# Modulation products of a two-block transformer kernel: units of 1 MB and pairs of 2 MB, and the stages beside which they stand

## The chip, the core and the metric

The kernel runs on one core of a Trainium2 chip. The metric is the device time of one execution in microseconds; three runs were taken of the kernel before, and one execution was profiled by itself. The engines are TensorE (PE, with its weight loads as PEld), VectorE (DVE), ScalarE (ACT), GpSimd (POOL) and SyncE (SP, which issues nearly all the transfers).

## What is computed

Two transformer blocks of two layers each work on 256 latent tokens and, in the first layer, on 256 context tokens of width 1024. Each layer takes six modulation vectors from a conditioning vector: a product with a 1024 x 6144 matrix, 24 MB in float32. Cut to what matters here:

```python
def modulation(cond, w_ada, b_ada):
    m = jax.nn.silu(cond) @ w_ada + b_ada
    return [t[..., None, :] for t in jnp.split(m, 6, axis=-1)]

for i in range(DEPTH):                       # first block
    sh1, sc1, g1, sh2, sc2, g2 = modulation(c, w_ada[i], b_ada[i])
    h = modulate(rms_norm(x, norm1_g[i]), sh1, sc1)
    x = x + g1 * (mixer(h) @ w_out[i])       # windowed, differential attention, gMLP
    x = x + g2 * conv_ffn(modulate(rms_norm(x, norm2_g[i]), sh2, sc2),
                          w_up[i], conv_w[i], conv_b[i], w_down[i])

for i in range(DEPTH):                       # second block
    m = (sc @ w_mod[i] + b_mod[i]).reshape(B, N_MOD, D_MODEL)
    # layer 0: attention with 8 heads; layer 1: multi-scale pooling
    # then conv_ffn_2, each behind a modulated norm and gated
```

The modulation weights of all four layers are 96 MB, a third of what the kernel reads.

## The kernel before

Everything is kept with features on the partitions: `x` is 128 x 8 x 256. Every other product is made of float32 weights split into a high and a low part: `fetch` (L203) loads a 1 MB chunk, ACT casts it to the high part (L238), DVE subtracts for the low part (L240), and `mms` (L270) issues three products per tile (high by high, high by low, low by high: L285, L286, L289). The modulation product is done in plain float32 and needs no split.

**The stages.** The first layer runs its mixer and its feed-forward for both streams (512 columns), the second layer and the second block for the latent stream alone (256 columns). Each feed-forward (`ffn`, L986) has 22 up-projections, each followed by a convolution (L978, L981, L983; in the first block of both the gate and the value half), and down-projections in groups that are interleaved with the ups.

**The modulation units.** A unit (`mod_part`, L400) is a quarter of one of the six vectors: 1 MB of weights, eight matmuls with 32 stationary columns (L410) into four quarters of one accumulator `acc`. They show in the trace as 16 records. The quarter's sum is put into `msum`: copied by ACT for the first quarter (L414), added by DVE for the others (L416). After the fourth, two transposes (L425) and one addition (L427) write the vector. `acc` is a PSUM tag with two buffers, which the down-projections, the output projections and the projections of the mixers use too, in turn.

**Their loads.** `mod_load` (L362) takes either one 1 MB buffer of the pool `x8` (seven buffers of 8 KB per partition, shared with activations and with every third split weight chunk), or two of three half-megabyte buffers `mw`. `mod_units` (L431) makes a list of steps: step q issues the matmuls of unit q - `ahead` and then the load of unit q.

**What sets the order.** PE and SP run in the program's order (`manual_schedule`, L1360). `spread` (L80) puts a list of steps evenly between the steps of a stage; `Line` (L33) holds generators with costs and due times, and lets their second halves follow when they are due. SP issues transfers in order, and each waits until its buffer has been read. Beside which stage the units stand is written in four places: `fill_a` (L1323), beside the first layer's mixer; `fill_f` (L1330), beside a feed-forward; the line `if l == 1` in `block1` (L945), beside the second layer's mixer; and `attention2` (L1241), beside the second block's attention. The last twelve units of the fourth layer stand in `self.late` (L1443).

```python
def fill_f(self, i):
    if i == 0:
        return self.more_units((1, 0, 12), x8=True)
    return self.more_units((2, 8, 24)) if i == 1 else []
...
        if l == 1:
            seq = seq[:12] + spread(seq[12:], self.more_units((1, 12, 24), (2, 0, 8)))
```

Of the kernel before, what the change touches and what calls it, by code (L numbers as in the profile page):

```python
# [79 lines left out]
def spread(main, fill):  # L80

    out, done = [], 0
    for i, u in enumerate(main):
        out.append(u)
        want = len(fill) * (i + 1) // len(main)
        out += fill[done:want]
        done = want
    return out + fill[done:]
# [3 lines left out]
WAIT = dict(b00=6, b01=5, b10=5.5, b_pv=2.5, c00=5, c01=5, c10=5, c_norm=1.5, c_pv=4,   # L92
            gmlp=3.5, gmlp_end=2, mod=1, norm=1.2, norm1=3, pool_out=4.5, qk0=4,
            qk0_first=10, qk1=4, qk1_first=8, qk2=4, s=6, s_pv=1.5)
# [11 lines left out]
class Stack:  # L106
# [201 lines left out]
    def go(self, gen, name=None):  # L308
        self.n += 1
        name = name or f"#{self.n}"  # L310
        self.line.start(name, gen)
        return name
# [84 lines left out]
        nc.vector.tensor_tensor(m, m, b.unsqueeze(2).to_broadcast([P, 2, 2]), ALU.add)  # L397
        yield 0.22, 0

    def mod_part(self, i, n, then=None):  # L400


        nc = self.nc
        j, q = divmod(n, 4)
        cpad = self.cpad
        acc = self.psum("acc", [P, 512])[:, :256]
        w = self.wm.pop((i, n))
        for e in range(2):
            for u in range(4):
                nc.tensor.matmul(acc[32 * u:32 * u + 32], lhsT=cpad[:, 2 * q + e], rhs=w[e][:, 256 * u:256 * u + 256],  # L410
                                 start=e == 0, stop=e == 1)
        if q == 0:
            self.msum[i, j] = self.mp.tile([P, NT], F32, tag="msum", name="msum", bufs=1)
            nc.scalar.copy(self.msum[i, j], acc)  # L414
        else:
            nc.vector.tensor_tensor(self.msum[i, j], self.msum[i, j], acc, ALU.add)  # L416
        if then is not None:
            then()
        yield 0.9, WAIT["mod"] if q == 3 else 0
        if q < 3:  # L420
            return
        sb = self.msum.pop((i, j))
        tr = self.psum("tr", [P, 2, 4, 32])
        for t in range(2):
            nc.tensor.transpose(tr[:, t].rearrange("p u v -> p (u v)"), sb[:, P * t:P * t + P], self.ident)  # L425
        b = self.sm(f"sm{i}", "b")[:, KD * j:KD * j + KD].rearrange("p (u t) -> p t u", t=2)
        nc.vector.tensor_tensor(self.mod[i][:, j].rearrange("p (u t) v -> p t u v", t=2), tr[:, :, :, i // 2 * 2:i // 2 * 2 + 2],  # L427
                                b.unsqueeze(3).to_broadcast([P, 2, 4, 2]), ALU.add)
        yield 0.22, 0

    def mod_units(self, ns, x8=False, ahead=1):  # L431

        def step(q):
            load = (lambda: self.mod_load(*ns[q], x8)) if q < len(ns) else (lambda: None)
            if q >= ahead:
                yield from self.mod_part(*ns[q - ahead], load)
            else:
                load()

        return [lambda q=q: self.go(step(q), "m%d.%d" % ns[q - ahead] if q >= ahead else None)  # L440
                for q in range(len(ns) + ahead)]

    def mods(self, i, j):

# [251 lines left out]
    def block1(self, l, after):  # L696
        nc, key, line = self.nc, f"sm{l}", self.line
# [4 lines left out]
        t = self.x8("kvqc")  # L702
        kTB, vB = t[:, 0:512], t[:, 512:1024].rearrange("p (k c) -> p k c", k=4)
        qTC = t[:, 1024:2048].rearrange("p (s a t) -> p s a t", s=2, a=2)
        t = self.x8("kvc")
# [3 lines left out]
        u, gk = uv[:, 0], f"gn{l}"  # L709
# [17 lines left out]
        def chunk(ci, post, ss):  # L727
            return [lambda s=s: self.go(self.proj(f"win{l}", ci, s, post), f"c{ci}{s}") for s in ss]
# [184 lines left out]
        need = lambda *names: [lambda: line.ensure(*names)]  # L913
        rev = streams[::-1]
        fill = self.fill_a(l)
        seq = chunk(0, post_bkv, (0,)) + chunk(1, post_bq(0), (0,)) + chunk(0, post_bkv, (1,))
        if l == 0:
            seq += chunk(1, post_bq(0), (1,))
        else:
            seq = seq[:2] + need("n1") + [self.last_loads] + seq[2:]  # L920
# [4 lines left out]
        n = len(streams)  # L925
# [16 lines left out]
        for a, b in MOVES[l]:  # L942
            seq.insert((a + b) % len(seq), seq.pop(a % len(seq)))
        if l == 1:
            seq = seq[:12] + spread(seq[12:], self.more_units((1, 12, 24), (2, 0, 8)))  # L945
        for u_ in seq:
            u_()
        if l == 1:
# [232 lines left out]
    def attention2(self):  # L1181
        nc, i, line = self.nc, 2, self.line
        kT, v = self.kT, self.v2
        self.qk_wait = WAIT["qk2"]
        qT = self.x8("qT").rearrange("p (a t) -> p a t", a=8)
        t = self.sx[:, 4:8].rearrange("p k t -> p (k t)")
# [50 lines left out]
        need = lambda *names: [lambda: line.ensure(*names)]  # L1237
        kx, vx = chunk(0, lambda acc, s: self.post_k(acc, s, tk)), chunk(1, self.post_v)
        q = [chunk(2 + c, post_q(c)) for c in range(4)]
        un = units()  # L1240
        f = self.more_units((3, 0, 12), x8=True, ahead=2)  # L1241
        seq = f[:1] + kx + vx + f[1:2] + q[0] + q[1] + need("c0", "c1", "c2")
        seq += spread(un[0], f[2:5]) + q[2] + need("c3") + spread(un[1], f[5:8]) + q[3] + need("c4")
        seq += spread(un[2], f[8:11]) + need("c5") + spread(un[3], f[11:])
        seq += need(*(f"a{hp}1" for hp in range(4)))
        for u in seq:
            u()
# [82 lines left out]
    def fill_f(self, i):  # L1330

        if i == 0:
            return self.more_units((1, 0, 12), x8=True)
        return self.more_units((2, 8, 24)) if i == 1 else []

    def more_units(self, *parts, **kw):
        return self.mod_units([(i, n) for i, a, b in parts for n in range(a, b)], **kw)
# [278 lines left out]
```

## Time and profile before

| | us |
|---|---|
| three runs, median (lowest to highest) | 1776.91 (1774.46 to 1777.22) |
| the profiled execution, its own time | 1774.65 |
| its span in the trace | 1772.9 |
| PE busy in the span | 1618.3 (91%) |
| DVE busy | 1195.8 (67%) |
| ACT busy | 878.9 (50%) |
| POOL busy | 135.2 (8%) |
| read from memory | 285.21 MB, 161 GB/s over the span |

The stages, by the first and last instructions of each: the first layer's mixer to 323 us, the first feed-forward 323 to 722, the second layer's mixer 722 to 941, the second feed-forward 941 to 1163, the second block's attention 1163 to 1301, the third feed-forward 1317 to 1500, the pooling mixer to 1570 and the fourth feed-forward to the end. A busy share is an average over a stretch in which matmuls overlap, so a stage with PE at 98% may still issue slowly; the granted clock of a stretch (PEclk) is 1.00 at 2.4 GHz and 0.50 at 1.2 GHz. What a stage waits for is read from its own waits, and not from the shares.

### The profile page before, as it was taken

Reading aid. Unit: us, or ns where it says so; the run is one execution under the profiler, and the core shown is the slowest. Engines: PE = TensorE matmul, PEld = TensorE weight load, DVE = VectorE, ACT = ScalarE, POOL = GpSimd, SP = SyncE. Lnnn points to the kernel's source line nnn. Section 1 sums busy time; section 2 is a strip of 40 time slices with the busy share of each in tenths; the row PEclk is TensorE's granted clock in tenths of the full one; section 3 lists DMA queues with packets and bytes.
Section 4 is the critical chain, followed back from the end, with each engine's and each line's share of the span. In section 5 each row is a group of like instructions: output and inputs, shape, how many; then the busy total and the mean of one; then the engine's idle time right before and its main releaser. Section 6 shows DMA issues by size and latency. Waiting matters only on the chain.

```text
span 1772.9 us, 32420 instructions
## 1 busy us (share of the span) xinstructions
PE 1618.3 (91%) x12604; PEld 1427.0 (80%) x12604; DVE 1195.8 (67%) x2903; ACT 878.9 (50%) x2147; POOL 135.2 (8%) x162
## 2 busy tenths in 40 slices
PE   7999797999999999898879999998979999779997
PEld 5878456989899898875468898886769999569997
DVE  5775786755564557876667768676786567886565
ACT  5343654533332343455345556454556565656563
POOL 0000001000000000000000001000141011431110
PEclk9999898999999999898989999999989999889998
DMA  7344331334333422245645776657455546435452
GB/s 308 119 143 143 124 107 49 130 109 142 113 127 120 142 97 98 89 139 203 227 143 192 254 256 233 209 189 263 166 182 188 176 176 210 179 119 212 157 187 87
DMA packets 71435, 288.36 MB, mean 163 GB/s; under 512 B 8177, under 2 KB 9457, under 8 KB 62577
## 3 DMA queue, kind: packets, MB, share of 16 engines
q1 hardware_dynamic: 69696, 283.91, 46.3%
q10 hardware_dynamic: 1584, 2.38, 0.4%
q8 instruction: 99, 1.62, 0.4%
q14 instruction: 56, 0.45, 0.1%
HBM read 285.21 MB, written 1.05 MB: 161 GB/s over the span
## 4 chain that ended last, share of the span: by engine, by line
PE 63%; DVE 17%; DMA 10%; ACT 6%; issue 3%; POOL 1%; SPq 0%; ACTq 0%; DVEq 0%; POOLq 0%
PE S L285 9%; PE S L286 9%; PE S L289 9%; PE acc L285 8%; PE acc L286 8%; PE acc L289 8%; DVE wl L240 5%; DMA w<-in_wup_dram 4%; PE acc L410 3%; DMA w<-in_wdn_dram 2%; ACT wh L238 2%; PE tr L661 2%; DVE ht L519 1%; DVE mx L651 1%; DMA mw<-in_wmod_dram 1%
## 5 line engine op out<-in xcount | busy, mean ns | idle before, releaser
L240 DVE TENSOR_TENSOR wl<-w,wh 128x384 fp32r<-128x384 f32 (+2 forms) x1010 | 489.6, 524 | 247.7 <-ACT wh L238 219.5
L238 ACT CAST wh<-w 128x384 fp32r<-128x384 f32 (+2 forms) x1010 | 419.7, 475 | 316.0 <-PE S L286 86.9
L285 PE MATMUL S<-hH,wh 128*128 128x256 f32 x1408 | 352.0, 287 | 25.7 <-ACT hH L529 17.4
L286 PE MATMUL S<-hL,wh 128*128 128x256 f32 x1408 | 349.8, 286 | 3.9 <-POOL hL L527 3.2
L285 PEld LDWEIGHTS S<-hH,wh 128*128 128x128 f32 x1408 | 272.3, 193 | 33.1 <-ACT hH L529 18.1
L286 PEld LDWEIGHTS S<-hL,wh 128*128 128x128 f32 x1408 | 272.0, 193 | 6.3 <-POOL hL L527 4.2
L285 PE MATMUL acc<-gH,wh 128*128 128x256 f32 (+1 forms) x728 | 208.6, 310 | 15.3 <-DVE xc L970 6.5
L286 PE MATMUL acc<-gL,wh 128*128 128x256 f32 (+1 forms) x728 | 205.4, 306 | 0.0
L289 PE MATMUL S<-hH,wl 128*128 128x256 f32 x1408 | 198.7, 284 | 0.0
L289 PEld LDWEIGHTS S<-hH,wl 128*128 128x128 f32 x1408 | 182.9, 193 | 0.0
L285 PEld LDWEIGHTS acc<-gH,wh 128*128 128x128 f32 x728 | 138.9, 191 | 30.6 <-ACT wh L238 5.4
L289 PE MATMUL acc<-gH,wl 128*128 128x256 f32 (+1 forms) x728 | 145.9, 306 | 0.0
L286 PEld LDWEIGHTS acc<-gL,wh 128*128 128x128 f32 x728 | 139.1, 191 | 5.9
L289 PEld LDWEIGHTS acc<-gH,wl 128*128 128x128 f32 x728 | 110.4, 191 | 6.4
L285 PE MATMUL acc<-wh,hH 128*128 128x256 f32 x344 | 92.7, 300 | 11.7 <-ACT hH L529 10.5
L981 DVE SCALAR_TENSOR_TENSOR cgv<-S,sm,cgv 128x255 f32<-128x255 f32 (+1 forms) x132 | 74.8, 567 | 39.7 <-ACT cgv L978 39.1
L1019 POOL TENSOR_TENSOR gL<-cgv,gH 128x256 fp32r<-128x256 f32 x66 | 50.5, 766 | 615.1 <-ACT gH L1018 595.7
L978 ACT ACTIVATE cgv<-S,sm 128x256 f32<-128x256 f32 (+1 forms) x132 | 82.9, 628 | 27.6 <-PE S L289 27.6
L970 DVE SCALAR_TENSOR_TENSOR x<-acc,mod,x 128x256 f32<-128x256 f32 x104 | 50.1, 481 | 61.1 <-PE acc L289 60.7
L286 PE MATMUL acc<-wl,hH 128*128 128x256 f32 x344 | 89.2, 290 | 0.0
L286 PE MATMUL S<-hcL,wh 128*128 128x256 f32 x352 | 86.5, 284 | 0.3 <-DVE hcL L530 0.3
L285 PE MATMUL S<-hcH,wh 128*128 128x256 f32 x352 | 86.4, 281 | 0.0
(268 smaller groups left out, 2873.1 us busy)
## 6 DMA issues: line engine op xcount, KB each, us to landing
w<-in_wup_dram SPq DMA_DIRECT2D x140, 512.0 KB, 3.8
mw<-in_wmod_dram SPq DMA_DIRECT2D x104, 512.0 KB, 4.8
wm<-in_wmod_dram SPq DMA_DIRECT2D x44, 1024.0 KB, 7.6
w<-in_wdn_dram SPq DMA_DIRECT2D x56, 512.0 KB, 3.7
w<-in_wup_dram SPq DMA_DIRECT2D x18, 1024.0 KB, 7.5
w<-in_win_dram SPq DMA_DIRECT2D x32, 512.0 KB, 4.0
w<-in_wout_dram SPq DMA_DIRECT2D x16, 512.0 KB, 5.2
w<-in_wqkv_dram SPq DMA_DIRECT2D x16, 512.0 KB, 4.2
```

What stands on the lines that cost most here:

```text
L238: self.nc.scalar.copy(h[:, c:d], w[:, c - a:d - a])
L240: self.nc.vector.tensor_tensor(l[:, c:d], w[:, c - a:d - a], h[:, c:d].bitcast(F32), ALU.subtract)
L285: mm(o, lhsT=s[0], rhs=m[0], start=k == ks[0], stop=False)
L286: mm(o, lhsT=s[0], rhs=m[1], start=False, stop=False)
L289: mm(o, lhsT=S(b, k)[1], rhs=M(b, k)[0], start=False, stop=end and k == ks[-1])
L410: nc.tensor.matmul(acc[32 * u:32 * u + 32], lhsT=cpad[:, 2 * q + e], rhs=w[e][:, 256 * u:256 * u + 256], start=e == 0, stop=e == 1)
L519: nc.vector.scalar_tensor_tensor(t, self.xs[s][:, ft], A, r, ALU.mult, ALU.mult)
L661: self.nc.tensor.transpose(tr[:, k], src[:, P * k:P * k + P], self.ident)
L970: self.nc.vector.scalar_tensor_tensor(x, acc[:, c], self.mods(i, j)[:, ft, s:s + 1], x, ALU.mult, ALU.add)
L978: nc.scalar.activation(out, ps, AF.Identity, scale=cw[:, n + f:n + f + 1], bias=cb[:, f:f + 1])
L981: nc.vector.scalar_tensor_tensor(o[:, :, 1:256], x[:, :, 0:255], cw[:, f:f + 1], o[:, :, 1:256], ALU.mult, ALU.add)
L1019: (nc.vector if T == 512 else nc.gpsimd).tensor_tensor(gL[:, a], c[:, 1, :T], gH[:, a].bitcast(F32), ALU.subtract)
```

## The change

`mod_part` becomes `mod_parts`: it takes `m` units that follow each other and multiplies them into one accumulator, which is evacuated once. With `m=2` a step is a pair: 2 MB, sixteen matmuls, one copy or addition. `mod_units` takes every `m`-th unit, loads `m` units per step and names a step by its last unit. Forty units, twenty pairs, stand beside the first feed-forward; the second layer's mixer keeps eight single units; the second feed-forward has none; the twelve beside the second block's attention become six pairs with a look-ahead of one step where it was two. The units of the first layer's mixer and the late ones stay single.

```diff
-    def mod_part(self, i, n, then=None):
+    def mod_parts(self, i, n, m, then=None):
         nc = self.nc
         j, q = divmod(n, 4)
         acc = self.psum("acc", [P, 512])[:, :256]
-        w = self.wm.pop((i, n))
-        for e in range(2):
+        ks = range(2 * q, 2 * (q + m))
+        ws = [w for a in range(m) for w in self.wm.pop((i, n + a))]
+        for k, w in zip(ks, ws):
             for u in range(4):
-                nc.tensor.matmul(acc[32 * u:32 * u + 32], lhsT=cpad[:, 2 * q + e], rhs=w[e][:, 256 * u:256 * u + 256],
-                                 start=e == 0, stop=e == 1)
+                nc.tensor.matmul(acc[32 * u:32 * u + 32], lhsT=self.cpad[:, k], rhs=w[:, 256 * u:256 * u + 256],
+                                 start=k == ks[0], stop=k == ks[-1])
...
-        yield 0.9, WAIT["mod"] if q == 3 else 0
-        if q < 3:
+        end = q + m == 4
+        yield 0.9 * m, WAIT["mod"] if end else 0
+        if not end:
             return
...
-    def mod_units(self, ns, x8=False, ahead=1):
+    def mod_units(self, ns, m=1, x8=False, ahead=1):
+        ns = ns[::m]
+        def load(q):
+            for a in range(m if q < len(ns) else 0):
+                self.mod_load(ns[q][0], ns[q][1] + a, x8)
         def step(q):
-            load = (lambda: self.mod_load(*ns[q], x8)) if q < len(ns) else (lambda: None)
             if q >= ahead:
-                yield from self.mod_part(*ns[q - ahead], load)
+                yield from self.mod_parts(*ns[q - ahead], m, lambda: load(q))
             else:
-                load()
+                load(q)
...
         if l == 1:
-            seq = seq[:12] + spread(seq[12:], self.more_units((1, 12, 24), (2, 0, 8)))
+            seq = seq[:12] + spread(seq[12:], self.more_units((1, 12, 20)))
...
-        f = self.more_units((3, 0, 12), x8=True, ahead=2)
-        seq = f[:1] + kx + vx + f[1:2] + q[0] + q[1] + need("c0", "c1", "c2")
-        seq += spread(un[0], f[2:5]) + q[2] + need("c3") + spread(un[1], f[5:8]) + q[3] + need("c4")
-        seq += spread(un[2], f[8:11]) + need("c5") + spread(un[3], f[11:])
+        f = self.more_units((3, 0, 12), x8=True, m=2)
+        seq = f[:1] + kx + vx + q[0] + q[1] + need("c0", "c1", "c2")
+        seq += spread(un[0], f[1:3]) + q[2] + need("c3") + spread(un[1], f[3:4]) + q[3] + need("c4")
+        seq += spread(un[2], f[4:6]) + need("c5") + spread(un[3], f[6:])
...
         if i == 0:
-            return self.more_units((1, 0, 12), x8=True)
-        return self.more_units((2, 8, 24)) if i == 1 else []
+            return self.more_units((1, 0, 12), (2, 0, 8), (1, 20, 24), (2, 8, 24), x8=True, m=2)
+        return []
```

The order on SP beside the first feed-forward, from the first down-projection weights on. `w` are the half chunks that are split, `wm` the 1 MB modulation loads. Before:

```order
L224 DMA w<-in_wdn_dram 128x1024 x4
L366 DMA wm<-in_wmod_dram 128x2048
L224 DMA w<-in_wup_dram 128x1024 x4
L366 DMA wm<-in_wmod_dram 128x2048
L224 DMA w<-in_wup_dram 128x1024 x4
L366 DMA wm<-in_wmod_dram 128x2048
```

Now:

```order
L366 DMA wm<-in_wmod_dram 128x2048 x2
L224 DMA w<-in_wdn_dram 128x1024 x4
L224 DMA w<-in_wup_dram 128x1024 x2
L366 DMA wm<-in_wmod_dram 128x2048 x4
L224 DMA w<-in_wup_dram 128x1024 x2
L366 DMA wm<-in_wmod_dram 128x2048 x2
L224 DMA w<-in_wup_dram 128x1024 x4
```

Where one load stood for every four half chunks of weights, there are now two or four, and the half chunks of the second next up-projection stand behind the four.

The order on PE in the middle of the second layer's mixer, where the first attention's scores (`S` from `qTB`) give way to the second's (`S` from `kvc`). `tr<-cst,Pm` are the transposes that wait for a softmax, L410 the modulation matmuls. Before:

```order
L410 MATMUL acc<-mw,cpad 32x256 x16
L839 MATMUL S<-kvc,kvqc 128x512 x2
L661 MATMUL tr<-cst,Pm 128x128 x8
L773 MATMUL tr<-ut,wsT 128x128 x4
L410 MATMUL acc<-mw,cpad 32x256 x8
L661 MATMUL tr<-cst,Pm 128x128 x8
L839 MATMUL S<-kvc,kvqc 128x512 x2
L425 MATMUL tr<-cst,msum 128x128 x2
L783 MATMUL tr<-cst,oa 128x128 x4
L661 MATMUL tr<-cst,Pm 128x128 x4
L824 MATMUL tr<-PT,kvqc 64x256 x8
L410 MATMUL acc<-mw,cpad 32x256 x16
```

Now (the line numbers from `mod_units` on are ten higher, L671 is the former L661):

```order
L410 MATMUL acc<-mw,cpad 32x256 x8
L671 MATMUL tr<-cst,Pm 128x128 x8
L849 MATMUL S<-kvc,kvqc 128x512 x4
L783 MATMUL tr<-ut,wsT 128x128 x4
L671 MATMUL tr<-cst,Pm 128x128 x8
L410 MATMUL acc<-mw,cpad 32x256 x8
L793 MATMUL tr<-cst,oa 128x128 x4
L671 MATMUL tr<-cst,Pm 128x128 x4
L834 MATMUL tr<-PT,kvqc 64x256 x8
L671 MATMUL tr<-cst,Pm 128x128 x4
L849 MATMUL S<-kvc,kvqc 128x512 x2
L410 MATMUL acc<-mw,cpad 32x256 x8
```

Five units stood in this piece, two of them twice directly behind another; now three stand in it, each by itself.

## Rows read from the trace of the kernel before

**Rows 1.** The page, the chain that ended last, by engine.
```profile
PE 63%; DVE 17%; DMA 10%; ACT 6%; issue 3%; POOL 1%; SPq 0%; ACTq 0%; DVEq 0%; POOLq 0%
```
**Rows 2.** Stretches: length, busy us (instructions) of PE, PEld, DVE, ACT, POOL; PEclk, DMA share, GB/s.
```profile
323.00:722.00 399.00, 391.09 (x2889) 360.95 (x2888) 237.74 (x491) 149.62 (x318) 0.00 (x0) 0.99 0.35 118
722.00:941.00 219.00, 188.75 (x1419) 143.66 (x1419) 155.87 (x420) 104.59 (x265) 4.41 (x6) 0.89 0.48 165
941.00:1163.00 222.00, 211.58 (x1842) 198.46 (x1842) 157.34 (x362) 119.16 (x292) 17.22 (x22) 0.99 0.67 231
786.00:826.00 40.00, 38.79 (x332) 27.98 (x331) 24.87 (x65) 23.34 (x55) 0.00 (x0) 1.00 0.59 214
826.00:909.00 83.00, 64.48 (x496) 37.06 (x494) 52.42 (x132) 31.77 (x79) 0.00 (x0) 0.88 0.64 220
6.00:26.00 20.00, 15.05 (x102) 10.38 (x102) 8.91 (x28) 11.70 (x33) 0.00 (x0) 1.00 1.01 421
```
**Rows 3.** Line L410's matmuls in four stages: count, ns min/median/max, first and last start.
```profile
L410 PE MATMUL acc<-wm,cpad x192: 379/379/403, 387.5 to 691.5; 128*32 128x256 f32 x192
L410 PE MATMUL acc<-mw,cpad x320: 376/379/636, 793.7 to 907.0; 128*32 128x256 f32 x160
L410 PE MATMUL acc<-mw,cpad x256: 379/379/403, 968.8 to 1139.4; 128*32 128x256 f32 x128
L410 PE MATMUL acc<-wm,cpad x192: 376/379/404, 1204.1 to 1258.1; 128*32 128x256 f32 x192
```
**Rows 4.** Timeline of PE at three places: start us, duration, line, instruction [idle before <-releaser].
```profile
420.43 1.07 PE L410 MATMUL acc<-wm,cpad 128*32 128x256 f32 x16
421.43 0.38 PE L285 MATMUL S<-hH,wh 128*128 128x256 f32 x1
421.65 0.28 PE L286 MATMUL S<-hL,wh 128*128 128x256 f32 x1
421.77 0.28 PE L285 MATMUL S<-hH,wh 128*128 128x256 f32 x1
...
453.07 1.07 PE L410 MATMUL acc<-wm,cpad 128*32 128x256 f32 x16
454.80 0.47 PE L285 MATMUL acc<-gH,wh 128*128 128x512 f32 x1 [0.66 <-DVE xc L970]
455.11 0.39 PE L286 MATMUL acc<-gL,wh 128*128 128x512 f32 x1
455.34 0.39 PE L285 MATMUL acc<-gH,wh 128*128 128x512 f32 x1
...
1248.77 1.93 PE L410 MATMUL acc<-wm,cpad 128*32 128x256 f32 x32
1250.63 0.70 PE L1206 MATMUL S<-kv,qT 128*128 128x512 f32 x1
```
**Rows 5.** Tile wm over the whole span: its 1 MB transfers, issue to landing.
```profile
DMA to landing us min/median/max: 4.7/7.6/18.9
```
**Rows 6.** Line L978 (convolutions) in the second and in the third feed-forward: first and last start.
```profile
L978 ACT ACTIVATE cgv<-S,sm x44: 546/555/567, 943.8 to 1115.1; 128x256 f32<-128x256 f32 x44
L978 ACT ACTIVATE cgv<-S,sm x22: 557/561/567, 1321.1 to 1468.6; 128x256 f32<-128x256 f32 x22
```
**Rows 7.** Waits of PE, 941 to 1163 us: us in total, times, longest.
```profile
PE S L285 <- DVE cgv L983: 3.0, 4, 1.3
```
**Rows 8.** A stretch of the second feed-forward, columns as in rows 2.
```profile
1023.00:1115.00 92.00, 89.00 (x785) 83.46 (x784) 68.14 (x153) 53.61 (x133) 9.28 (x12) 1.00 0.65 224
```
**Rows 9.** Chain of waits within 820 to 910 us: shares by line; one piece.
```profile
by line: DMA mw<-in_wmod_dram 15.2%; PE acc L410 12.2%; PE tr L661 7.5%; PE S L839 6.9%; DMA w<-in_wout_dram 6.0%; DVE mx L651 5.2%; PE tr L824 4.3%; PE tr L863 4.3%; ACT Pm L846 3.5%; PE acc L285 3.1%; PE acc L286 2.9%; DVE wl L240 2.7%; P
...
826.72 5.16 DMA mw<-in_wmod_dram
```
**Rows 10.** Waits of PE, 786 to 909 us, columns as in rows 7.
```profile
PE acc L410 <- DMA mw<-in_wmod_dram: 11.0, 8, 3.6
PE tr L661 <- DVE Pm L851: 3.1, 3, 1.5
```

More of the change, by code (lines that the diff above doesn't have):

```diff
@@ L398, in mod_unit @@
         yield 0.22, 0
-    def mod_part(self, i, n, then=None):
+    def mod_parts(self, i, n, m, then=None):
         nc = self.nc
         j, q = divmod(n, 4)
-        cpad = self.cpad
         acc = self.psum("acc", [P, 512])[:, :256]
-        w = self.wm.pop((i, n))
-        for e in range(2):
+        ks = range(2 * q, 2 * (q + m))
+        ws = [w for a in range(m) for w in self.wm.pop((i, n + a))]
+        for k, w in zip(ks, ws):
             for u in range(4):
-                nc.tensor.matmul(acc[32 * u:32 * u + 32], lhsT=cpad[:, 2 * q + e], rhs=w[e][:, 256 * u:256 * u + 256],
-                                 start=e == 0, stop=e == 1)
+                nc.tensor.matmul(acc[32 * u:32 * u + 32], lhsT=self.cpad[:, k], rhs=w[:, 256 * u:256 * u + 256],
+                                 start=k == ks[0], stop=k == ks[-1])
         if q == 0:
@@ L426, in mod_part, with go @@
         b = self.sm(f"sm{i}", "b")[:, KD * j:KD * j + KD].rearrange("p (u t) -> p t u", t=2)
-        nc.vector.tensor_tensor(self.mod[i][:, j].rearrange("p (u t) v -> p t u v", t=2), tr[:, :, :, i // 2 * 2:i // 2 * 2 + 2],
+        nc.vector.tensor_tensor(self.mod[i][:, j].rearrange("p (u t) v -> p t u v", t=2),
+                                tr[:, :, :, i // 2 * 2:i // 2 * 2 + 2],
                                 b.unsqueeze(3).to_broadcast([P, 2, 4, 2]), ALU.add)
         yield 0.22, 0
-    def mod_units(self, ns, x8=False, ahead=1):
+    def mod_units(self, ns, m=1, x8=False, ahead=1):
[3 more added lines that the diff above has]
+                self.mod_load(ns[q][0], ns[q][1] + a, x8)
         def step(q):
-            load = (lambda: self.mod_load(*ns[q], x8)) if q < len(ns) else (lambda: None)
             if q >= ahead:
-                yield from self.mod_part(*ns[q - ahead], load)
+                yield from self.mod_parts(*ns[q - ahead], m, lambda: load(q))
             else:
-                load()
-        return [lambda q=q: self.go(step(q), "m%d.%d" % ns[q - ahead] if q >= ahead else None)
-                for q in range(len(ns) + ahead)]
+                load(q)
+        def go(q):
+            i, n = ns[q - ahead] if q >= ahead else (0, 0)
+            self.go(step(q), f"m{i}.{n + m - 1}" if q >= ahead else None)
+        return [lambda q=q: go(q) for q in range(len(ns) + ahead)]
     def mods(self, i, j):
```

## The prediction

> **What bounds the kernel now.** I read the page first: its chain of waits, followed back from the last instruction, is 63% TensorE (PE) work, 17% VectorE (DVE), 10% transfers [rows 1]. A stage is thus judged by what PE does in it. The table of stretches [rows 2] gives that: in the first feed-forward (323 to 722 us) PE is busy 391 of 399 us at clock 0.99 and the transfers move 118 GB/s. In the second layer's mixer (722 to 941) it is busy 189 of 219 at clock 0.89, at 165 GB/s; in the second feed-forward (941 to 1163) 212 of 222, at 231 GB/s. The change takes 12 of 20 units out of the mixer and all 16 out of the second feed-forward, and puts 28 more beside the first. The counts are 16 records a unit: 192, 320, 256 and 192 in four stages [rows 3], so 12, 20, 16 and 12 units.
>
> So PE work goes from two stages that wait to one that doesn't. What it costs there is PE time; what it gives back is PE time plus the waits that stand around the units. Both must be priced.
>
> **A unit and a pair.** A single unit takes 1.00 us from its first matmul to the next instruction's (420.43 to 421.43), and two units back to back 1.86 (1248.77 to 1250.63) [rows 4]. Entering one costs a little more than the 0.12 us pitch of the stream it interrupts (421.65 to 421.77); I put 1.09 for a unit and 1.95 for a pair. The back-to-back units there have two accumulators; I see no reason for a pair with one to differ, and take the same. A pair is also evacuated once instead of twice; that work is VectorE's and ScalarE's, which have idle time in every stage concerned (VectorE 68 of 92 us busy where it is busiest [rows 8]), and is costed at nothing.
>
> **First feed-forward.** Twenty pairs at 1.95 come (39.0), twelve units at 1.09 go (13.1). A unit between two down-projections is now followed by a wait of 0.66 us for VectorE's residual, since the accumulators alternate and a unit is too short to cover it (453.07, then 454.80) [rows 4]. A pair is 0.86 us longer, so that wait is covered; if half of the twelve have it, 4.0 go. The closing transposes move with the units and cancel in the sum. **+22 us**, PE being on the path all through.
>
> Does a load hold PE up there? A pair's 2 MB lie in two buffers of the pool `x8`; the new order on SP, shown with the change, has four 1 MB loads in a row beside each group of downs. Each waits until PE has read its buffer, and SP's later weight loads queue behind it. Between two fills in a down group stand three downs. A 512-column matmul takes 0.23 us (455.11 to 455.34) [rows 4], so a down of twelve takes 2.7, three 8.2; with half a pair on each side a buffer is free about 9 us before its next use. A 1 MB load on an idle queue lands after 4.7 us [rows 5]; while many queue up the transfers run at 421 GB/s (6 to 26 us) [rows 2], 2.5 us per MB, so both megabytes land after 4.7 + 2.5 = 7.2 us. That fits, with 2 us to spare. The weight load behind them is needed only after the rest of the group and one more up-projection (over 11 us), so it costs nothing. I take 0 and keep for the range 2.5 us, one more transfer in front, at each of the ten narrow places: +25.
>
> **Second feed-forward.** From its first to its last gate convolution, 44 of them, it takes 943.8 to 1115.1 = 171.3 us. The same stretch of the third feed-forward (the same 22 up-projections, the same eight downs, no units) takes 1321.1 to 1468.6 = 147.5 [rows 6]. The difference, 23.8, is twelve units at 1.09 (13.1) and 10.7 of waits. This layer has a second convolution per up-projection, so the 3.0 us in which PE waits for it [rows 7] may stay: 20.8 go. Of the 47 us left, four units go, 4.4. **-25 us.** The lower end is the 16 units' own time, 17 us, if every wait stays because VectorE or the weight loads set the pace. VectorE is busy 74% there [rows 8], so it is near but isn't the bound. The upper end is 28: no wait stays.
>
> **Second layer's mixer.** Twelve units at 1.09 go: 13. Then the waits: the chain through 820 to 910 us is 15.2% transfers of modulation weights and 6.0% of output weights queued behind them, some 13.7 and 5.4 of 90 us, one piece alone 5.2 us [rows 9]. PE itself waits 11.0 us for them in eight places [rows 10]. The reason is spacing: units stand up to two in a row and the three half-megabyte buffers come free only as PE reads them. In the new order eight units stand with softmax work between each two, so I let 9 of the 11 go. Against that stands what the units covered: with fewer of them PE comes sooner to transposes that wait for softmax, which already cost 3.1 us in three places [rows 10]. I put +6, half the cover that is gone. The clock: the stretch 826 to 909 has 0.88 [rows 2], so 24% of 83 us at 1.2 GHz, the lower of its two levels, about 10 us lost; the first half, 786 to 826, with no long wait, has 1.00. I let 4 of the 10 return. **-13 - 9 + 6 - 4 = -20 us**; ends -6 (the freed cover turns wholly into waits, the clock stays) and -30.
>
> Here a page speaks against the change. The clock row says that PE fell to half rate where it waited for transfers. The Trainium skill, TensorE: Matmul & The Clock Gate, section "HAM oscillation — how this bites in real kernels", says that idle gaps between groups of matmuls send the array back to half rate, so taking filler matmuls away from a stage with gaps invites it. By that rule the 4 us wouldn't return and more would be lost; by the row, the falls followed transfer waits that go. I follow the row and keep the rule's outcome as a rival.
>
> **Second block's attention.** Six pairs for twelve units: 6 x (2.18 - 1.95) = 1.4 saved, some of it in waits for a pair's second megabyte. **-1 us**, ends -2 and +3.
>
> **Sum.** +22 - 25 - 20 - 1 = -24 us on the profiled execution's 1774.65: **1751 us**. The profiled execution lies 2.3 us under the median of the runs shown, 1776.91; I don't add that. All other stages keep their instructions.
>
> **Rivals.**
> *The units only move.* Their own time goes with them and every wait returns elsewhere: +22 - 17 - 13 - 1 = -9, **1766 us**. For it: the largest wait of PE in the second feed-forward is for VectorE's convolution [rows 7], not for a unit. Against it: the third feed-forward, which shows the stage without units at 147.5 us.
> *The mixer at half clock* (the other side). PE is busy 64.5 of the 83 us from 826 to 909 at mean clock 0.88 [rows 2], 56.7 us at full rate; without eight units 48. At 1.2 GHz throughout that is 96, with 8 of waits 104 instead of 83: +21, less 4 in the first half. Total +22 - 25 + 17 - 1 = +13, **1788 us**. It decides once the granted clock there falls under about 0.6 (48/0.58 + 8 = 91, the stretch 8 us longer than now, at which the sum is zero). Against it: 786 to 826 held 1.00 with much the same mixture.
> *Pairs arrive late in the first feed-forward.* Ten narrow places at 2.5 us: the gain is gone, **1776 us**. For it: the loads are issued at the last moment, from one queue. Against it: 7.2 us against 9.
>
> **How the numbers follow.** Forecast 0.62, its own range 1744 to 1764: the ends of the three gains lie 8, 14 and 4 above their values and 3, 10 and 1 below, and I take half of each sum; units only move 0.20; late pairs 0.10; half clock 0.08. A measurement here tells 0.2% from no change, 3.6 us. Faster: nearly all of the first, most of the second, a third of the third: 0.81. Same: 0.07. Slower: the half clock and the bad end of the late pairs, 0.12. The range reaches over the first two cases and leaves out some 0.18: **1737** (all lower ends together) **to 1771**.
>
> **What would show it.** Right: the first feed-forward some 421 us long, still over 97% PE, with no PE wait for the modulation tile; the second feed-forward near 197, its first to last convolution near 150; the mixer near 199 with a transfer wait of 2 us or less; 16-record groups replaced by 32-record groups of 1.86 us. Wrong: PE waits for modulation transfers in the first feed-forward (late pairs); the second feed-forward still over 205 (units only move); a granted clock under 0.8 from the attention's middle to its end.

## The result, and the profile after

| | us |
|---|---|
| kernel before, four runs, median (lowest to highest) | 1776.2 (1774.46 to 1777.22) |
| changed kernel, four runs, median (lowest to highest) | 1757.85 (1754.48 to 1758.66) |
| ratio, 95% interval | 0.9894 (0.9877 to 0.9911) |
| changed kernel, the profiled execution, its own time | 1754.48 |
| its span | 1752.7 |

Faster by 1.1%; 1751 was forecast. The two profiled executions are 20.2 us apart, -24 was the sum of the terms. The chain of waits by engine answers to [rows 1]; its shares say little, since some stages grew and others shrank:

```profile
PE 61%; DVE 18%; DMA 10%; ACT 7%; issue 3%; POOL 1%; SPq 0%; ACTq 0%; DVEq 0%; POOLq 0%
```

So near a sum could come from terms that are all right, or from errors that cancel. A cut by stages tells which. I cut at two kinds of event that both kernels have: the first gate convolution of a feed-forward (before L978, now L988) and the last matmul of its last down-projection. Each feed-forward then holds all the units that stand beside it, and each mixer what lies between. The table of stretches of the kernel before, cut so (columns as in [rows 2]); its four rows are the first feed-forward, the second layer's mixer, the second feed-forward, and the second block's attention:

```profile
327.70:717.30 389.60, 381.69 (x2818) 351.55 (x2817) 229.57 (x472) 145.38 (x307) 0.00 (x0) 0.99 0.35 119
717.30:943.90 226.60, 196.35 (x1475) 151.26 (x1475) 162.12 (x435) 107.32 (x273) 4.41 (x6) 0.89 0.48 163
943.90:1160.90 217.00, 206.58 (x1804) 193.75 (x1802) 153.19 (x351) 118.38 (x291) 17.22 (x22) 0.99 0.67 232
1160.90:1321.10 160.20, 137.80 (x1036) 110.98 (x1036) 120.06 (x290) 83.07 (x206) 27.41 (x32) 0.93 0.58 205
```

The same four stages of the changed kernel:

```profile
324.90:741.00 416.10, 410.36 (x3280) 365.96 (x3279) 234.68 (x482) 149.18 (x314) 0.00 (x0) 1.00 0.49 183
741.00:934.80 193.80, 170.93 (x1275) 138.80 (x1273) 155.72 (x422) 105.47 (x270) 4.43 (x6) 0.94 0.38 124
934.80:1138.40 203.60, 189.39 (x1539) 186.54 (x1540) 151.25 (x337) 117.72 (x288) 19.00 (x22) 0.98 0.50 171
1138.40:1300.90 162.50, 137.06 (x1037) 111.21 (x1036) 116.83 (x281) 82.23 (x206) 27.47 (x32) 0.94 0.55 197
```

Read the second column, the length, against the forecast: first feed-forward +26.5 (forecast +22), mixer -32.8 (-20), second feed-forward -13.4 (-25), attention +2.3 (-1). The part ahead of the first convolution, in which no instruction changed, was 2.8 us shorter. The sum is near because two errors cancel: in this pair of traces the mixer gave 13 us more than I put and the second feed-forward 12 less, both beyond the ends I had kept.

**First feed-forward.** A pair as PE's timeline shows it between two down-projections (start, length in us, what, number of records):

```profile
470.87 0.61 PE L289 MATMUL acc<-gH,wl 128*128 128x512 f32 x2
471.42 1.93 PE L410 MATMUL acc<-wm,cpad 128*32 128x256 f32 x32
473.28 0.50 PE L285 MATMUL acc<-gH,wh 128*128 128x512 f32 x1
```

471.42 to 473.28 is the 1.86 us that the prediction had. What PE waited for in this stage (us in total, times, longest), first in the kernel before, then in the changed one:

```profile
PE acc L285 <- DVE xc L970: 6.5, 4, 4.8
```

```profile
PE acc L285 <- DVE xc L980: 4.8, 1, 4.8
PE acc L410 <- DMA wm<-in_wmod_dram: 0.9, 1, 0.9
```

One wait of 4.8 us at the stage's end is in both. Of the waits behind a short unit, 1.7 us in three places went, where I had put 4.0 in six. The pairs' loads are late once, by 0.9 us. With those sizes the term is 39.0 - 13.1 - 1.7 + 0.9 = 25.1. PE's timeline, added up from each matmul's start to the next one's, has it otherwise: the units' matmuls with the waits behind them went from 15.6 to 38.4 us, the closing transposes, which I had let cancel, from 0.4 to 1.4, and the down-projections' matmuls from 131.4 to 133.5. Why the last grew is open.

**Mixer.** PE's waits in the changed kernel, the five largest:

```profile
PE tr L671 <- DVE Pm L861: 5.6, 2, 3.3
PE acc L285 <- ACT wh L238: 3.6, 1, 3.6
PE tr L620 <- DVE rp L649: 2.8, 2, 1.9
PE S L849 <- ACT Pm L817: 2.8, 1, 2.8
PE acc L285 <- ACT mixH L266: 2.8, 1, 2.8
```

The 11.0 us of transfer waits [rows 10] are gone without a rest, and the softmax waits (`Pm`) grew from 3.1 to 8.4, near the 6 that were put. PE's idle time, length less busy, went from 30.3 to 22.9 us, -7.4. The other 25.4 us are PE's busy time, 196.35 to 170.93. Twelve units are 13.1 of it, which leaves 12.3. The clock column can account for them: at 0.89, 22% of 226.6 us were spent at 1.2 GHz, 50 us; at 0.94, 12% of 193.8, 23 us. If PE is busy all through, 27 us less at half rate are some 13 us of work, where I had let 4 return. One pair of traces doesn't carry that far, though. The run b_ff2_only (below) leaves these twenty units where they were, and its mixer ran at 0.93:

```profile
733.50:956.40 222.90, 189.57 (x1472) 145.22 (x1471) 160.78 (x434) 107.33 (x273) 4.41 (x6) 0.93 0.50 165
```

From there to the changed kernel PE's busy time falls by 18.6 us, 5.5 more than the units. In the changed kernel the clock fell five times in this stage, each time beside or right behind one of the waits of 1.9 to 3.6 us listed above (the fall at 846.6 us from the span's start, for one, beside the wait of 2.8 for `Pm`). None of these waits is for a transfer.

**Second feed-forward.** From first to last gate convolution it took 166.7 us, where I expected 150 and had 171.3. PE's waits there:

```profile
PE S L285 <- DVE cgv L993: 6.7, 7, 1.2
PE S L285 <- ACT wh L238: 4.9, 2, 4.4
```

The units are gone, and with them 17.2 us of PE's busy time (206.58 to 189.39); its idle time grew by 3.8, since PE waits for the convolution more than before (6.7 for 3.0, [rows 7]). For the cast of weights it waits 4.9 us, as before (5.0). The traces alone don't say what paces the stage now. That is what most of the experiments are about.

### The profile page after: what moved, and what is told of

Same layout as the page of the kernel before. It is cut to its first block, busy times and chain, and to the rows that moved or that the text cites. A ratio compares the mean times of both kernels' runs of the same rounds, so it can differ in the third digit from the quotient of the medians.

```text
span 1752.7 us, 32334 instructions
## 1 busy us (share of the span) xinstructions
PE 1599.5 (91%) x12604; PEld 1419.1 (81%) x12604; DVE 1188.5 (68%) x2877; ACT 879.1 (50%) x2147; POOL 136.7 (8%) x162
## 4 chain that ended last, share of the span: by engine, by line
PE 61%; DVE 18%; DMA 10%; ACT 7%; issue 3%; POOL 1%; SPq 0%; ACTq 0%; DVEq 0%; POOLq 0%
PE S L285 9%; PE S L286 9%; PE S L289 9%; PE acc L285 8%; PE acc L286 8%; PE acc L289 8%; DVE wl L240 6%; DMA w<-in_wup_dram 5%; PE acc L410 3%; ACT wh L238 2%; DMA w<-in_wdn_dram 2%; DVE ht L529 1%; PE tr L671 1%; DMA wm<-in_wmod_dram 1%; DVE mx L661 1%
## 5 line engine op out<-in xcount | busy, mean ns | idle before, releaser
L988 ACT ACTIVATE cgv<-S,sm 128x256 f32<-128x256 f32 (+1 forms) x132 | 82.7, 628 | 47.3 <-PE S L289 47.3
L285 PE MATMUL acc<-wh,hH 128*128 128x256 f32 x344 | 91.2, 296 | 10.4 <-ACT hH L539 8.2
```

Of the source, the lines that this page charges most:

```text
L285: mm(o, lhsT=s[0], rhs=m[0], start=k == ks[0], stop=False)
L988: nc.scalar.activation(out, ps, AF.Identity, scale=cw[:, n + f:n + f + 1], bias=cb[:, f:f + 1])
```

## The experiments

The stages of every profiled run, cut as above, in us; each stands in one execution. "Share" means units beside the mixer / beside the second feed-forward.

| run | share | first f.-f. | mixer | clock in it | second f.-f. |
|---|---|---|---|---|---|
| before | 20 / 16 | 389.6 | 226.6 | 0.89 | 217.0 |
| changed | 8 / 0 | 416.1 | 193.8 | 0.94 | 203.6 |
| i_change_again | 8 / 0 | 415.6 | 198.6 | 0.91 | 200.5 |
| a_mixer_only | 8 / 16 | 397.5 | 191.5 | 0.95 | 217.5 |
| b_ff2_only | 20 / 0 | 404.0 | 222.9 | 0.93 | 201.1 |
| h_all_first | 0 / 0 | 426.3 | 194.0 | 0.89 | 203.2 |
| e_third_buffer | 8 / 0 | 414.6 | 191.9 | 0.95 | 186.6 |
| k_third_buffer_again | 8 / 0 | 415.0 | 192.2 | 0.95 | 186.8 |
| j_buffer_and_ff2_units | 8 / 16 | 397.1 | 191.7 | 0.95 | 216.2 |
| c_singles | 8 / 0 | 427.9 | 195.3 | 0.94 | 202.2 |
| d_one_conv | 8 / 0 | 415.6 | 196.6 | 0.93 | 187.9 |
| f_pool_mult | 8 / 0 | 416.9 | 199.2 | 0.90 | 203.1 |
| g_mixer_x8 | 20 / 0 | 403.4 | 233.3 | 0.89 | 200.7 |
| l_mixer_ahead | 20 / 0 | 403.2 | 233.3 | 0.89 | 201.0 |

One execution is not exact to a microsecond: the part ahead of the first feed-forward, the same instructions in all these, took 322.4 to 331.4 us, and the mixer with eight units 191.5 to 199.2. Differences of stages under 5 us are not argued from.

### Each half of the move alone

a_mixer_only:

```diff
-            return self.more_units((1, 0, 12), (2, 0, 8), (1, 20, 24), (2, 8, 24), x8=True, m=2)
-        return []
+            return self.more_units((1, 0, 12), (2, 0, 8), (1, 20, 24), x8=True, m=2)
+        return self.more_units((2, 8, 24)) if i == 1 else []
```

> Only the twelve units of the second layer's mixer are moved (as pairs, with the twelve that stood beside the first feed-forward: twelve pairs there); the sixteen beside the second feed-forward stay there as single units. Theory (the second feed-forward is paced by its weights' way through load, ScalarE's cast and VectorE's subtraction, so units there stand in PE's gaps): the first feed-forward is 8 x 1.95 = 15.6 us shorter than in the changed kernel, the second feed-forward's first to last gate convolution goes from 166.7 back to about 171; sum -11, about 1747 us. Rival (sixteen units cost 16 x 1.09 = 17.4 us of PE time wherever they stand): about 1760 us.

Measured: 1751.76 us, ratio to the kernel before 0.9832 (0.979 to 0.9875), the changed kernel's being 0.9894 (0.9877 to 0.9911); the two all but touch, and the changed kernel's second measurement, 0.9864 to 0.9923 (i_change_again), overlaps, so "at least as fast" is what this shows. The total came out between the two expectations, and by other stages than mine: the second feed-forward went back to 217.5, not to 208 (the 171 expected between the convolutions and the changed kernel's 37 behind them), so sixteen units there cost 14 us, 0.87 each; and the first feed-forward was 18.6 us shorter, 2.3 a pair, not 1.95. By the stages, moving these sixteen costs at least what it gains.

b_ff2_only:

```diff
-            return self.more_units((1, 0, 12), (2, 0, 8), (1, 20, 24), (2, 8, 24), x8=True, m=2)
+            return self.more_units((1, 0, 12), (2, 8, 24), x8=True, m=2)
...
-            seq = seq[:12] + spread(seq[12:], self.more_units((1, 12, 20)))
+            seq = seq[:12] + spread(seq[12:], self.more_units((1, 12, 24), (2, 0, 8)))
```

> Only the sixteen units of the second feed-forward are moved (fourteen pairs beside the first feed-forward); the mixer keeps its twenty units. Theory (moving these sixteen gains next to nothing): against the kernel before +27.3 (14 pairs at 1.95) - 13.1 - 4 in the first feed-forward, -5 to -8 in the second, -1 in the attention: +1 to +5, about 1779 us. Rival (the second feed-forward's gain is there and was given back by the mixer's change): +10 - 21 to -25, about 1763 us.

The mixer kept all its twenty units, not twelve as the expectation says. Measured: 1773.15 us, 0.9957 (0.9925 to 0.9989), between the two. First feed-forward +14.4, second -15.9: an exchange. The ratio leaves 0.4% for this half with its pairs, 0.8% at most; a_mixer_only has 1.7% without it. Most of the gain of the whole change is thus the mixer's twelve units.

### Pairs or singles

c_singles:

```diff
-            return self.more_units((1, 0, 12), (2, 0, 8), (1, 20, 24), (2, 8, 24), x8=True, m=2)
+            return self.more_units((1, 0, 12), (2, 0, 8), (1, 20, 24), (2, 8, 24), x8=True)
...
-        f = self.more_units((3, 0, 12), x8=True, m=2)
+        f = self.more_units((3, 0, 12), x8=True, ahead=2)
```

(with the attention's order of the kernel before, for single units)

> All units stand where the changed kernel has them, but one by one: forty single units beside the first feed-forward, twelve beside the attention. Theory (a pair saves the second entry and the wait for the other accumulator behind a unit that is too short to cover it): 20 x (2.18 - 1.95) = 4.6 us, and up to 20 waits of 0.66 us, 13: 1763 to 1775 us, with PE waits for VectorE's residual in the first feed-forward. Rival (pairing is worth nothing, only the place counts): within 2 us of the changed kernel, 1756 to 1760 us.

Measured: 1767.3 us, 0.9919 (0.9889 to 0.9948). The first feed-forward took 427.9 us, 11.8 more than with pairs: a pair saves 0.59 us. Of that, 4.5 us are the waits:

```profile
PE acc L285 <- DVE xc L980: 9.3, 8, 4.8
```

Eight for one, 4.5 us more. For this stage the theory holds, with 7.3 us for the entries where 4.6 were put; in the whole time the interval overlaps the changed kernel's. In the attention pairs and singles can't be told apart (161.7 here; 158.6 to 165.2 in the runs with pairs and two weight buffers), so the -1 there is neither shown nor refuted.

### What paces the second feed-forward

Two rows of the changed kernel suggest an answer. A half-megabyte load of up-weights lands 4.4 us after its issue (the transfers' view, 27 loads); then come a cast of 0.51 and three subtractions of 0.57 before the buffer is free for the next. That makes a round of 6.6 us, estimated from these rows, without what else ScalarE and VectorE do in between. Two buffers hold the two halves of a chunk, so without the chunks that go through `x8` an up-projection could come every 6.6 us, while its 48 matmuls need 48 x 0.12 = 5.8. The alternative is the amount of work on VectorE and ScalarE.

d_one_conv:

```diff
-            if i < 2:
+            if i < 1:
                 self.conv(c[:, 1, :T], ps[:, 1, :T], key, KF + j)
```

> The changed kernel, with the second layer's value half not convolved (the second feed-forward then multiplies the gate by the raw projection, as the third and fourth do: one activation and two VectorE operations less per up-projection). Theory (VectorE and ScalarE set that stage's pace, by the second convolution that stands between the weights' casts and subtractions): first to last gate convolution falls from 166.7 to about 148 us, as in the third feed-forward, and the time to about 1740 us. Rival (the transfers of the weights set the pace, half chunks queued behind whole ones): it stays over 160 us and the time over 1752.

This kernel leaves out a part of the layer, so it is good for this measurement alone. Measured: 1743.87 us, 0.9798 (0.975 to 0.9846); first to last gate convolution 148.4. So the second convolution is the difference between this stage and the third feed-forward, as expected to the microsecond. It does not tell work from round: taking operations from ScalarE and VectorE shortens both.

f_pool_mult:

```diff
-                nc.vector.tensor_tensor(c[:, 1, :T], c[:, 0, :T], c[:, 1, :T], ALU.mult)
+                (nc.gpsimd if i else nc.vector).tensor_tensor(c[:, 1, :T], c[:, 0, :T], c[:, 1, :T], ALU.mult)
```

> The changed kernel with the second feed-forward's product of gate and value (22 operations, 0.42 us each, 9 us) on GpSimd instead of VectorE. Theory B (VectorE's work sets that stage's pace): first to last gate convolution falls from 166.7 by about 7, to 160 us, and the time to about 1751. Theory A (the round of the two weight buffers): it stays at 165 to 168, the time within 2 us of the changed kernel's.

Measured: 1757.84 us, 0.9873 (0.9824 to 0.9923); 167.1 us between the convolutions. That is what Theory A gave, but the run does not prove it, because VectorE got no time back. Its groups of the subtraction in that stage (line, engine, operation, tiles, count, busy time and mean ns), of the changed kernel and then of this run:

```profile
L240 DVE TENSOR_TENSOR wl<-w,wh 128x384 fp32r<-128x384 f32 x109 | 59.1, 569 | 24.2 <-ACT wh L238 24.2
```

```profile
L240 DVE TENSOR_TENSOR wl<-w,wh 128x384 fp32r<-128x384 f32 x109 | 64.1, 620 | 29.6 <-ACT wh L238 29.2
L1024 POOL TENSOR_TENSOR cgv<-cgv 128x256 f32<-128x256 f32 x21 | 16.4, 783 | 275.5 <-ACT wh L238 209.9 <-DVE cgv L993 59.8 <-ACT cgv L988 5.8
```

With 21 more operations on GpSimd the subtraction's mean rose from 569 to 620 ns. The Trainium skill, SBUF — State Buffer, section "Who interferes with whom", says that a VectorE instruction with two SBUF inputs contends with a GpSimd instruction that reads SBUF; both are that here, and the trace agrees, with 51 ns.

e_third_buffer and k_third_buffer_again (one kernel, the second time in more runs):

```diff
-                w = self.wp.tile([P, CH // 2], F32, tag="w", name="w", bufs=2)
+                w = self.wp.tile([P, CH // 2], F32, tag="w", name="w", bufs=3)
...
-            w = self.mp.tile([P, 1024], F32, tag="mw", name="mw", bufs=3)
+            w = self.mp.tile([P, 1024], F32, tag="mw", name="mw", bufs=2)
...
-            b = self.wp.tile([P, 4, 256], F32, tag="w", name="b", bufs=2)
+            b = self.wp.tile([P, 4, 256], F32, tag="w", name="b", bufs=3)
```

> The changed kernel with three instead of two half-megabyte buffers for raw weights; the room comes from the modulation buffers, two instead of three, which can cost time in both mixers, so the second feed-forward is read by itself. Theory A (the pace of the second feed-forward is the round of a buffer: load, cast, subtraction, next load): first to last gate convolution falls from 166.7 to about 150 us. Theory B (the pace is what VectorE and ScalarE have to do per up-projection): it stays over 161 us.

> The three-buffer version of the changed kernel once more, with more rounds. Theory (the buffer's round was a wait in the second feed-forward and, less so, in the attention and the later feed-forwards): 1724 to 1731 us, a ratio to before of 0.969 to 0.973, and 29 to 32 us under the changed kernel on the same chip. Rival (a lucky chip in the first two runs): over 1738.

Measured: 1727.19 us in two runs, 0.9709 (0.9661 to 0.9757), then 1728.69 in five, 0.9745 (0.9721 to 0.977). First to last gate convolution 150.8, then 151.2. On one chip with the changed kernel (1755.18) it is 26.5 us faster, a little less than the 29 to 32 expected. VectorE has the same work as before: 151.66 us busy in the stage, now of 186.6 instead of 203.6.

```profile
936.90:1123.50 186.60, 184.49 (x1540) 183.91 (x1541) 151.66 (x337) 117.33 (x288) 18.84 (x22) 1.00 0.53 187
```

So it is the round of the buffer, with the second convolution in it, and not the amount of work: with two buffers but one convolution (d_one_conv) PE was busy 184.25 of 187.9 us, too. What the operations on the raw weights waited for, and who waited for them, between the convolutions (the view of tile `w`), first in the changed kernel, then here:

```profile
its engine sat idle before it (us, times) until:
  ACT wh L238: 24.2, 25
  DMA w<-in_wup_dram: 21.1, 14
  PE acc L286: 8.5, 2
  PE S L289: 3.8, 1
...
who waited for it (us, times):
  DVE wl L240: 24.2, 25
  ACT wh L238: 20.9, 18
  PEld S L285: 9.2, 6
  PE S L285: 4.9, 2
```

```profile
its engine sat idle before it (us, times) until:
  ACT wh L238: 12.6, 13
  PE acc L286: 8.5, 2
  PE S L286: 7.0, 7
  DMA w<-in_wup_dram: 6.3, 7
...
who waited for it (us, times):
  DVE wl L240: 12.6, 13
  ACT wh L238: 4.6, 6
  PEld S L285: 1.9, 3
  PE S L285: 0.6, 2
```

The wait for the landing falls from 21.1 to 6.3 us and that for the casts from 24.2 to 12.6, while the waits for PE grow from 12.3 to 15.5: PE has become the slower one. PE is at 99% with the clock at 1.00. The attention gained too (155.9 and 159.0), and the third and fourth feed-forwards 2 to 4 us each. This version beats both kernels.

j_buffer_and_ff2_units is the third buffer together with a_mixer_only's edit: sixteen units beside the second feed-forward again.

> Three raw-weight buffers (two modulation buffers), and the second feed-forward keeps its sixteen single units, so that only the mixer's twelve are moved. Theory (with the third buffer PE is the bound of the second feed-forward, so a unit costs its own 1.09 us there): that stage, first convolution to last down-projection, is 17 us longer than without them (186.6 to about 204), the first feed-forward 17 to 18 us shorter: within 3 us of the three-buffer run, about 1727. Rival (gaps are left that units fill): stage under 197, time about 1718. Second rival (their loads between the weights' delay these as before): stage over 210, time over 1734.

Measured: 1740.5 us, 0.9822 (0.9799 to 0.9846), 12 us slower than the three-buffer version without those units on the same chip. The numbers are the second rival's, 216.2 us for the stage and not 204; its mechanism is not shown. The stage's row, and what PE and SP waited for there:

```profile
920.20:1136.40 216.20, 206.68 (x1804) 193.69 (x1805) 151.72 (x356) 120.14 (x292) 19.71 (x22) 0.99 0.68 239
```

```profile
PE S L285 <- DVE cgv L993: 2.8, 3, 1.4
PE acc L410 <- DMA mw<-in_wmod_dram: 2.8, 3, 1.5
PE acc L285 <- DVE x L980: 2.5, 1, 2.5
```

```profile
SPq L372 <- PE acc L410: 78.3, 12, 10.4
```

SP stood 78.3 us on modulation loads that wait for PE to read their buffer (60.8 in a_mixer_only), and the next weight loads are behind them in its order. But PE's matmuls wait for no cast of weights any more (5.0 us in the kernel before), so late weights can be no large part of it. Of the 29.6 us by which the stage is longer than without units, 22.2 are PE's busy time, where 17 were put, and 7.4 idle time. So the four corners of this stage are 217.0 (units, two buffers), 216.2 (units, three), 203.6 (none, two) and 186.6 (none, three). With the units PE is busy 95% already, its idle time 10.4 us with two buffers and 9.5 with three; without them the third buffer takes it from 14.2 to 2.1. These units have two instead of three modulation buffers in j, and PE's 2.8 us of waits for their transfers were not there before; how much of the 12 us above 204 that makes was not tried.

### The mixer

g_mixer_x8 and l_mixer_ahead, both on b_ff2_only's placement:

```diff
-            seq = seq[:12] + spread(seq[12:], self.more_units((1, 12, 24), (2, 0, 8)))
+            seq = seq[:12] + spread(seq[12:], self.more_units((1, 12, 24), (2, 0, 8), x8=True))
```

> Only the second feed-forward's units are moved, as in the run before that left the mixer alone (1773 us), and the mixer's twenty units load through the 1 MB buffers instead of the three of half a megabyte. Theory (of the mixer's gain, 29 us against that run, the transfer waits of 11.8 us and what follows them are a part that has nothing to do with the units' place): PE's waits for modulation transfers fall under 3 us, the mixer from 222.9 to about 211, the time to about 1762. Rival (the waits come from the units standing too close, whatever the buffers): the waits stay over 8 us, the mixer over 219, the time over 1770.

and, in l, `x8=True, ahead=2`:

> As the run whose mixer kept its twenty units and loaded them through 1 MB buffers, but two units ahead instead of one. Theory (the mixer's waits come from a load that is issued only behind the unit before it, not from the units' number): waits for modulation transfers fall from 19.9 to under 5 us, the mixer from 233 to 212 to 217. Rival (transfers queue up, whatever their order): waits over 10 us, the mixer over 222.

Measured: 1783.19 us, 1.0026 (1.0004 to 1.0047), and 1775.08, 1.0007 (0.9984 to 1.003); the mixer 233.3 in both. PE's waits for modulation transfers, 11.8 us in b_ff2_only, did not fall, in g and then in l, followed by what SP's loads waited for in l:

```profile
PE acc L410 <- DMA wm<-in_wmod_dram: 19.9, 7, 4.9
```

```profile
PE acc L410 <- DMA wm<-in_wmod_dram: 17.1, 7, 4.9
```

```profile
SPq L224 <- DVE wl L240: 106.5, 15, 21.2
SPq L366 <- PE acc L410: 55.1, 16, 12.0
```

Both theories of mine fell, and the times are those of the rivals. Asking earlier doesn't help: SP then stands 55.1 us on loads whose `x8` buffer still holds an earlier unit, and 106.5 us (94.1 in the kernel before) on raw weights, behind which the units' loads queue. Which of the two makes PE wait, these runs don't tell. Twenty units here wait in every form that I tried, eight don't wait at all.

h_all_first takes the last eight away too:

```diff
-            return self.more_units((1, 0, 12), (2, 0, 8), (1, 20, 24), (2, 8, 24), x8=True, m=2)
+            return self.more_units((1, 0, 12), (1, 12, 20), (2, 0, 8), (1, 20, 24), (2, 8, 24), x8=True, m=2)
...
-            seq = seq[:12] + spread(seq[12:], self.more_units((1, 12, 20)))
+            pass
```

> The changed kernel with the mixer's last eight units also beside the first feed-forward (24 pairs there, none beside the mixer). Theory (a unit left in the mixer stands alone and costs its own 1.09 us): the mixer falls by 8.7, the first feed-forward rises by 4 x 2.1 = 8.4: within 3 us of the changed kernel, 1758. Rival A (each costs there what the twelve did, 2.4 us and more): mixer -20, the time about 1746. Rival B (they fill PE's gaps in the softmax part and cost nothing): mixer -2 or less, the time about 1764.

Measured: 1767.62 us, 0.9923 (0.9892 to 0.9955). Four pairs more cost 10.2 us in the first feed-forward and the mixer gave nothing back, 194.0 where the runs with eight units have 191.5 to 199.2: Rival B. Its mixer, and then that of i_change_again, the changed kernel on a second chip:

```profile
756.90:950.90 194.00, 167.98 (x1143) 139.92 (x1141) 153.49 (x413) 105.14 (x268) 4.43 (x6) 0.89 0.25 81
```

```profile
742.80:941.40 198.60, 174.55 (x1274) 142.35 (x1273) 155.89 (x421) 105.45 (x270) 4.42 (x6) 0.91 0.36 121
```

In h PE has some 130 matmul records less than the changed kernel and is idle 26.0 us instead of 22.9; 22% of the stage is at 1.2 GHz instead of 12%. So in this trace a part of what the units had cost came back as waits and a part as a slower clock. That is the rule which the prediction set against its own row: the Trainium skill, TensorE: Matmul & The Clock Gate, section "HAM oscillation — how this bites in real kernels", has gaps between groups of matmuls send the array back to half rate. For the last eight units the trace agrees with it, 0.89 against 0.94, but f_pool_mult, which has the eight, stands at 0.90, so the runs don't show it. For the first twelve the tendency is the other way: 0.89 to 0.93 in the four traces with twenty units, 0.90 to 0.95 in the nine with eight. The twenty brought 11.0 to 19.9 us of transfer waits, the eight none; that these waits held the clock down is not shown by itself.

> The changed kernel itself once more, on the chip of the three runs beside it. Every theory: a ratio to the kernel before of 0.988 to 0.991, some 1758 us; the second layer's mixer 190 to 200 us, according to how much of it the granted clock spends at half rate.

Measured: 1755.18 us, 0.9894 (0.9864 to 0.9923), the same ratio as the first time. Its row above shows the mixer at 0.91 and 198.6 us with the same instructions that took 193.8 at 0.94. So some 5 us of the mixer's gain in the first pair of traces belong to that one execution, 3.6 of them in PE's busy time. One trace of h, at 0.89, is no proof of the clock's part either; that moving the eight units gains nothing is borne out by the time, whose ratio is no better than the changed kernel's, though the intervals overlap.

## Why the prediction was right

**The total** was 7 us under the median and the range held it, partly by chance: in the profiled pair two terms were wrong by 12 to 13 us in opposite directions.

**First feed-forward, +22: +26.5.** The mechanism held: PE is busy 410.36 of 416.10 us, a pair takes 1.86, and its loads fit the gap (0.9 us late once, where the bound had 25). Mis-sized was "if half of the twelve have it, 4.0 go": three places, 1.7 us. That the closing transposes "cancel in the sum" holds for the total and not for this stage, where they added 1.0. And 1.95 doesn't hold for every further pair: from twelve pairs (a_mixer_only) to twenty-four (h_all_first) the stage grew by 28.8 us, 2.4 a pair.

**Second feed-forward, -25: -13.4 (-16.5 in the second execution), below the lower end of 17.** This step failed, and in it the sentence that VectorE "is near but isn't the bound", with only the 3.0 us of direct waits staying. VectorE's work is indeed not the bound. But its operations, and ScalarE's, stand inside the round by which a raw-weight buffer comes free, and the second convolution lengthens that round. The third feed-forward, my model, has no second convolution: without it this stage takes 148.4 instead of 166.7, and with a third buffer, convolution and all, 150.8. The price of units that I read from the comparison of the two stages was mostly this round. The rival "the units only move" was right for this stage: their own 17 us went, and waits grew by 3.8.

**Mixer, -20: -32.8, beyond the upper end of 30.** Units and transfer waits went as worked out, and the new softmax waits were as put. PE's idle time fell by 7.4, where 9 - 6 = 3 was put. The clock's term was mis-sized in this pair of traces, some 12 instead of 4. But it hangs on the execution: with the twenty units at 222.9 (b_ff2_only) or 226.6, and the changed kernel at 193.8 or 198.6, the gain is 24 to 33, and what PE's busy time lost beyond the units 2 to 12. So the 4 is not refuted, and the overshoot is in part luck of the two traces. The rival at half clock did not come (0.94, and 0.91). The falls of the clock that were left did not follow transfers, as the row had suggested, but other waits.

**Second block's attention, -1:** +2.3 in one execution, within the spread of the runs; open.

**Late pairs** did not come.

## What to carry to other kernels

When two stages look alike and one is slower, list all that differs between them before pricing one difference: here the faster stage had neither the units nor the second convolution, and most of the convolution's price ran through a buffer's round, not through a wait that bears its name. Two obstacles in one stage can hide each other: taking the units away gave 13 us, a third buffer beside them 1 (with a modulation buffer less), both 30, so a small gain does not say that the cause was wrong. Moving work out of a stage with gaps paid here as long as the work made waits itself; the eight units that made none were as good as free there, and moving them cost 10 us elsewhere.

## What the runs showed of the hardware

Moving 21 operations of 128 x 256 to GpSimd took none of VectorE's busy time away: its subtractions took 620 instead of 569 ns beside them, so that VectorE was busy 124.64 of 168 us against 125.12 of 167. In that run the 32 of these subtractions that overlapped an instruction on GpSimd took 791 ns in the mean, the others 549; in the changed kernel 21 did, at 648, and the others took 551. And the granted clock of a stage with gaps differs between executions of the same instructions: 0.94 and 0.91 for the changed kernel's mixer, 5 us apart, and 0.89 and 0.93 for the mixer with twenty units.
